# A seven-product unit in three accumulators, and a chunk's final products tied behind the accumulators' evictions

## The chip, the cores and the metric

The kernel runs on one core of one Trainium2 chip. The metric is the device time of one execution in microseconds (us), the median of several runs. Engines: PE is TensorE (matrix products into PSUM), DVE is VectorE, ACT is ScalarE, POOL is GpSimd, SP is SyncE, which here only issues DMAs. Each engine works through its own instructions in order.

## The reference

A trunk of two layers over x (1 x 2048 x 1024, float32), each `x <- x + mixer(RMSNorm(x))`, and a last RMSNorm. Layer A's mixer is a gated linear recurrence (RG-LRU) of width 1536. Layer B's is a short gated convolution:

```
u = einsum('bsd,dc->bsc', h, w_in)            # 1024 -> 4 x 1536
bg, cg, xv, gate = the four parts of u
y = bg * causal_depthwise_conv(cg * xv, conv_w)
out = einsum('bsc,cd->bsd', y * silu(gate), w_out)
```

Results must hold float32 accuracy; the kernel multiplies float32 as pairs of float16 (a high and a low part), three matmuls for one product.

## The kernel before, in words

All activations are held transposed, channels on the 128 partitions and 512 positions of the sequence along the row; such a 512-wide piece of the sequence is a chunk, two chunks a half. There are four chunks, 0 to 3.

Layer B's in-projection (`in_B`, `in_proj`, `unit`) makes 24 units of 256 output channels, each for both halves: 48 units. A unit is a 2 x 2 block product (output channels by chunks), done with seven block products instead of eight, after Strassen and Winograd: A11, S1, S2, A12, S4, S3 and A22 name the weight operand, and each meets one operand of the normalised x. A block product is four times three matmuls of 128x128 by 128x512, all into one PSUM accumulator (`product`, `mm3`). Accumulators come from a ring of six (`acc_tile`). The four results d[0,0], d[0,1], d[1,1], d[1,0] are sums of these products. Some sums are formed by letting further products grow in the same accumulator, others by adding an accumulator to a result in SBUF. Before, `unit` does it so:

- A11 grows in p; ACT copies p to d10 (L549). S1 is taken into r; DVE adds it to d10, giving d11 (`plus`, L539).
- The last product of the unit before is made here (`flush`): A22 grows in that unit's q, and DVE adds q to d10.
- S2 into a new q; DVE adds to d11, giving d01. A12 grows in p; ACT copies p to d00 (L565), which is finished.
- S4 into a new r; DVE adds it to d01, finished. S3 grows in q; DVE adds it to d11, finished. The final A22 in q waits for the next unit.

So a unit takes four accumulators, DVE evicts five times and ACT twice. A matmul that lets a product grow in an accumulator must wait until the eviction that reads the accumulator before it is over. Finished results go on to ACT (SiLU, L1020), POOL (products, L973 to L1049), and squares on ACT (L767, for the scale of the next operands).

Beside this, DVE and ACT split the next unit's weights into high and low halves (`split`, L420, L421), POOL forms the sums of weights (L484), and DVE does the convolution (L1005, L1009) and the evictions (L539).

Layer B's out-projection (`OutSums.run`) does the same seven products at a larger scale: for each half of the sequence, seven names, four row blocks q each, 28 products of 18 matmuls (6 operand blocks by 3). The first half's order is S1, S4, A12, A11, S2, S3, A22; the second's A11, S2, S3, A22, A12, S1, S4, the last two in half widths. A11, S2, S3 and A22 of one q grow in one accumulator. After each product DVE adds the accumulator to the residual x (`add_to_x`, L1428), one product late (`lag(1)`). Operands are loaded by SP (`fetch_to`) and split by ACT and DVE (L1117, L1118) some products ahead.

When all row blocks of a chunk are in, `endB` ends it: the sum of squares is turned into the factor `inv` of the last RMSNorm, and the chunk's eight blocks are multiplied with it (L1706), two of them on POOL and six on DVE, and stored. For chunks 0 and 1 `inv` is spread over the partitions by two DMAs issued from POOL's queue: `rd<-r` writes it to DRAM (L252), `inv<-rd` reads it back to all partitions (L253). In the first half chunk 1 is finished by S3's products and chunk 0 by A22's. The steps of an ending are put off by a count of products (`defer`, `tick`): for chunks 0 and 1 the sums at the fourth, the eight multiplications at the ninth (L1710).

What sets the order on an engine: the program is laid out when the kernel is built, by a simulation of time (`schedule_with_timeline_sim=True`) that takes instructions as they become ready in it, by priority. `after(a, b)` adds an order alone: a is laid out behind b, without any wait at run time. `evac_last` holds the last eviction of an accumulator; before, only the earlier out stage of layer A sets it.

Of the kernel before, what the change touches and what calls it, by code (L numbers as in the profile page):

```python
# [10 lines left out]
AF = mybir.ActivationFunctionType  # L11
ALU = mybir.AluOpType
# [34 lines left out]
def trunk(ctx, tc, xT, xn, prm, wa, ga, oa, wb, ob, out):  # L47
    nc = tc.nc
    v, s, g, sp = nc.vector, nc.scalar, nc.gpsimd, nc.sync
# [145 lines left out]
    def et(name, dt=F32):  # L195
        return buf(wk, "e", name, NE, dt)
# [95 lines left out]
    def inv_between(acc, inv, queue=None):  # L292

        ss = ps.tile([P, 4], F32, tag="g", name="ss", bufs=2)[:, 0 : acc.shape[1] // P]
        with tc.high_priority(PR):
            sums_of(acc, ss, pe_last[0])
        if not queue:
            yield
        with tc.high_priority(PR):
            inv_from(ss, inv, queue, s.copy, pe_last[0])  # L300
        yield
# [196 lines left out]
    def mm3(acc, wh, wl, xh, xl, start, stop, behind=None):  # L498
        kw = dict(skip_group_check=True)
        ins = nc.tensor.matmul(acc, wh, xh, start=start, stop=False, **kw)  # L500
        if behind is not None:
            after(ins, behind)
        nc.tensor.matmul(acc, wh, xl, start=False, stop=False, **kw)  # L503
        return nc.tensor.matmul(acc, wl, xh, start=False, stop=stop, **kw)  # L504

    throttle, pe_last, blocks_last, evac_last = [None, None], [None], [None], [None]
# [5 lines left out]
    def acc_tile(name):  # L512
        return ps.tile([P, CH], F32, tag="acc", name=name, bufs=6)
# [3 lines left out]
    def flush():  # L517

        while pending:
            pending.pop(0)()  # L520

    def unit(w, ops, dest, done, end):

        undo = w["undo"]

        def product(acc, wn, xn, start, stop):
            for k in range(4):
                kk = slice(k * P, (k + 1) * P)  # L530
                t, x = w[wn], ops[xn, k]
                pe_last[0] = mm3(
                    acc, t[:, 0, kk], t[:, 1, kk], x[:, 0, :], x[:, 1, :],
                    start and k == 0, stop and k == 3,
                )

        def plus(out, acc, t):
            with tc.high_priority(1000):
                ins = v.scalar_tensor_tensor(  # L539
                    out=out, in0=acc, scalar=undo, in1=t, op0=ALU.mult, op1=ALU.add  # L540
                )
            throttle[:] = ins, ins

        p = acc_tile("p")
        product(p, "A11", "B11", True, False)
        yield
        d10, d11 = dest(1, 0), dest(1, 1)
        with tc.high_priority(1000):
            s.activation(d10, p, AF.Copy, scale=undo)  # L549
        r = acc_tile("r")  # L550
        product(r, "S1", "T1", True, True)
        plus(d11, r, d10)
        yield
        if pending:
            flush()
            yield
        q = acc_tile("q")
        product(q, "S2", "T2", True, False)
        d01 = dest(0, 1)
        plus(d01, q, d11)  # L560
        yield
        product(p, "A12", "B21", False, True)
        d00 = dest(0, 0)
        with tc.high_priority(1000):
            s.activation(d00, p, AF.Copy, scale=undo)  # L565
        done(0, 0, d00)
        yield
        r = acc_tile("r")
        product(r, "S4", "B22", True, True)
        plus(d01, r, d01)  # L570
        done(0, 1, d01)
        yield
        product(q, "S3", "T3", False, False)
        plus(d11, q, d11)
        done(1, 1, d11)
        yield

        def last():
            product(q, "A22", "T4", False, True)
            plus(d10, q, d10)  # L580
            done(1, 0, d10)
            end()

        pending.append(last)
# [56 lines left out]
    def defer(fn, steps):  # L641
        deferred.append([steps, fn])

    def tick(n=1):

        for d in list(deferred):
            d[0] -= n
            if d[0] <= 0:
                deferred.remove(d)
                d[1]()  # L650
# [432 lines left out]
    def after(ins, first):  # L1083
        tc.add_manual_dep(
            ins.ins, first.ins.name,
            mybir.DependencyInfo(mybir.DependencyClass.NoSync, mybir.DependencyReason.SCHED_ONLY),
            reason="order",
        )
# [214 lines left out]
    class OutSums:  # L1303
# [98 lines left out]
        def run(self, emit, end_chunk, ending):  # L1402

            late = []

            def lag(n):
                while len(late) > n:
                    late.pop(0)()
                    next(ending, None)

            def product(acc, half, name, q, ts):
                start = SEVEN[name][2]
                for k in range(KH):
                    w, x = self.wops[name, k], self.zops[half, name, k]
                    kk = slice(q * P, (q + 1) * P)
                    behind = None if ts is CHUNK else last_of.get("PE")
                    mm = mm3(
                        acc[:, ts], w[:, 0, kk], w[:, 1, kk], x[:, 0, ts], x[:, 1, ts],
                        start and k == 0, k == KH - 1, behind,
                    )  # L1420
                    last_of["PE"] = mm
                throttle[:] = throttle[1:] + [mm]
                pe_last[0] = mm

            def add_to_x(acc, half, name, q, ts, final):
                m, c = SEVEN[name][1]
                x = self.x[half, m, c, q]
                ins = v.scalar_tensor_tensor(  # L1428
                    out=x[:, ts], in0=acc[:, ts], scalar=zsc[half][:, 2:3], in1=x[:, ts],
                    op0=ALU.mult, op1=ALU.add,  # L1430
                )
                if final:
                    cc, d = 2 * half + c, ND * m + q
                    if emit(cc, d, x, ts, ins):
                        end_chunk(cc, ts)

            n = 0
            for half, order in enumerate(self.ORDERS):
                accs = {}
                steps = [(name, CHUNK) for name in order]  # L1440
                if half:
                    steps[5:] = [(name, ts) for ts in (FIRST, SECOND) for name in order[5:]]
                for p, (name, ts) in enumerate(steps):
                    if (half, p) == (0, 3):
                        self.scales(1)
                    dest = SEVEN[name][1]
                    final = not [o for o, _ in steps[p + 1 :] if o != name and SEVEN[o][1] == dest
                                 and ts is CHUNK]
                    chain = ("S" if name in ("S1", "S4") else "Z" if name == "A12" else "X")
                    for q in range(ND):  # L1450
                        self.fetch_to(n)
                        while self.splits and self.splits[0][0] <= n:
                            self.split()
                        if SEVEN[name][2]:
                            accs[chain, q] = acc_tile("acc")
                        a = accs[chain, q]
                        product(a, half, name, q, ts)
                        late.append(
                            lambda a=(a, half, name, q, ts, final): add_to_x(*a)
                        )  # L1460
                        lag(1)
                        tick(1 if ts is CHUNK else 0.5)
                        n += 1 if ts is CHUNK else 0.5
                    if ts is not CHUNK:
                        lag(0)
                lag(0)
# [33 lines left out]
    acc = et("sa")  # L1500
# [11 lines left out]
    for c in range(2):  # L1512
        for i in range(4):
            t = wk.tile([P, D], F32, tag="xn", name="xn", bufs=4)
# [180 lines left out]
    def endB(c, ts):  # L1695
        if ts is not CHUNK:
            defer(lambda: endings.append(last_chunk(c, ts)), 1 if ts is FIRST else 0)
            return
        iv = et("inv")

        def ended():
            yield from inv_between(sums[c], iv, g if c < 2 else None)
            for d in range(KB):
                f = kept[c, d]
                eng = g if d % 3 == 2 else v
                eng.tensor_tensor(out=f, in0=f, in1=iv, op=ALU.mult)  # L1706
                sp.dma_start(out[d * P : (d + 1) * P, c * CH : (c + 1) * CH], f)

        steps = ended()
        for n in (4, 9) if c < 2 else (2, 3, 4):  # L1710
            defer(lambda: next(steps, None), n)


# [144 lines left out]
```

## Time and profile before

| | us |
|---|---|
| median of 3 runs | 1998.85 (1995.98 to 1999.11) |
| the profiled execution | 1997.66 |
| its span, first to last instruction | 1995.4 |
| PE busy | 1959.1 (98%) |
| DVE busy | 1257.5 (63%) |
| ACT busy | 1002.9 (50%) |
| POOL busy | 604.5 (30%) |
| mean granted TensorE clock | 0.994 |
| layer B's in-projection | about 868.8 to 1756.9 of the span |

Busy time is the time in which an engine's datapath works. Matmuls are pipelined and their ends are modelled, so single matmuls overlap in the records; the time from start to start is their pace. A wait is the idle time of an engine just before an instruction, with what ended it. In the rows below, times count from the span's start.

### The profile page before, as it was taken

To read this page: it belongs to the slowest core of one execution; us is meant where nothing else is said; L and a number is where in the kernel's file an instruction comes from. 1 tells how busy PE (TensorE), PEld (TensorE's weight loads), DVE (VectorE), ACT (ScalarE), POOL (GpSimd) and SP (SyncE) were. 2 spreads that over 40 slices of the span, in tenths; PEclk is the share of its full clock that TensorE was granted. 3 is DMA by queue.
4 is the path that set the end of the run, shared out by engine and by line. 5 is a ranking of instruction groups with operands and counts; after the bars stand their busy time and mean duration, and the time that the engine had idled before them with its cause. 6 is when DMAs were issued, how large, how long until landed. Compare 5 with 4: busy or idle time off the path is not lost.

```text
span 1995.4 us, 25154 instructions
## 1 busy us (share of the span) xinstructions
PE 1959.1 (98%) x9064; PEld 914.7 (46%) x9064; DVE 1257.5 (63%) x2137; ACT 1002.9 (50%) x1816; POOL 604.5 (30%) x486
## 2 busy tenths in 40 slices
PE   8999999999999999999999999999999999999988
PEld 3444444444444444444444444444444444444436
DVE  7977666667575745479647657658547438554455
ACT  7878786868584623155443343443432432435332
POOL 0001010101010311134553574664644544512221
PEclk9999999999999999999999999999999999999989
DMA  9111313052204824422141241232221120596442
GB/s 316 46 62 49 98 45 103 31 174 67 82 11 138 274 69 159 101 80 73 60 148 32 85 159 60 89 133 84 74 85 33 53 74 22 204 365 223 137 153 85
DMA packets 130957, 216.25 MB, mean 108 GB/s; under 512 B 13200, under 2 KB 41488, under 8 KB 130832
## 3 DMA queue, kind: packets, MB, share of 16 engines
q1 hardware_dynamic: 130384, 213.58, 32.4%
q8 instruction: 71, 1.16, 0.2%
q0 software_dynamic: 448, 1.06, 0.2%
q14 instruction: 54, 0.44, 0.1%
HBM read 152.19 MB, written 62.40 MB: 108 GB/s over the span
## 4 chain that ended last, share of the span: by engine, by line
PE 87%; DVE 6%; ACT 2%; DMA 2%; issue 2%; POOL 0%; SPq 0%; DVEq 0%; ACTq 0%; POOLq 0%
PE acc L500 14%; PE acc L503 14%; PE acc L504 14%; PE q L500 6%; PE q L504 6%; PE q L503 6%; PE p L504 4%; PE p L500 4%; PE p L503 4%; PE r L500 4%; PE r L504 4%; PE r L503 4%; PE pg L878 3%; DVE cg L1009 1%; DVE wc L421 1%
## 5 line engine op out<-in xcount | busy, mean ns | idle before, releaser
L503 PEld LDWEIGHTS <-wc 128*128 128x128 f16 x2096 | 205.1, 98 | 261.7 <-issue 27.5
L500 PEld LDWEIGHTS <-wc 128*128 128x128 f16 x2096 | 208.0, 99 | 253.3 <-issue 18.5
L504 PEld LDWEIGHTS <-wc 128*128 128x128 f16 x2096 | 205.2, 98 | 257.9 <-issue 14.5
L503 PE MATMUL acc<-op,wc 128*128 128x512 f16 x752 | 285.5, 380 | 2.8 <-DVE op L313 2.8
L504 PE MATMUL acc<-op,wc 128*128 128x512 f16 x752 | 285.7, 380 | 0.0
L500 PE MATMUL acc<-op,wc 128*128 128x512 f16 x752 | 283.3, 380 | 1.3 <-ACT op L311 1.3
L500 PE MATMUL q<-op,wc 128*128 128x512 f16 x576 | 216.5, 379 | 4.6 <-DVE ed L539 2.5
L903 POOL TENSOR_TENSOR u<-fixed,u 128x512 f32<-128x512 f32 x48 | 51.3, 1091 | 556.4 <-ACT fixed L900 556.4
L503 PE MATMUL q<-op,wc 128*128 128x512 f16 x576 | 218.3, 379 | 0.0
L504 PE MATMUL q<-op,wc 128*128 128x512 f16 x576 | 218.0, 379 | 0.0
L421 DVE SCALAR_TENSOR_TENSOR wc<-ws,fixed,wc 128x512 f16<-128x512 f32 x104 | 101.3, 979 | 87.6 <-ACT wc L420 79.5
L504 PE MATMUL p<-op,wc 128*128 128x512 f16 x384 | 145.5, 379 | 0.8 <-DVE wc L421 0.8
L503 PE MATMUL p<-op,wc 128*128 128x512 f16 x384 | 145.5, 379 | 0.0
L500 PE MATMUL p<-op,wc 128*128 128x512 f16 x384 | 145.5, 379 | 0.0
L500 PE MATMUL acc<-zs,wf 128*128 128x512 f16 x384 | 145.5, 379 | 0.0
L503 PE MATMUL acc<-zs,wf 128*128 128x512 f16 x384 | 145.5, 379 | 0.0
L504 PE MATMUL r<-op,wc 128*128 128x512 f16 x384 | 145.5, 379 | 0.0
L503 PE MATMUL r<-op,wc 128*128 128x512 f16 x384 | 145.5, 379 | 0.0
L500 PE MATMUL r<-op,wc 128*128 128x512 f16 x384 | 145.5, 379 | 0.0
L500 PE MATMUL acc<-op,wf 128*128 128x512 f16 (+1 forms) x384 | 136.2, 355 | 9.2 <-DVE xo L1428 9.2
L504 PE MATMUL acc<-zs,wf 128*128 128x512 f16 x384 | 145.2, 379 | 0.0
L503 PE MATMUL acc<-op,wf 128*128 128x512 f16 (+1 forms) x384 | 136.1, 354 | 0.0
(197 smaller groups left out, 3507.2 us busy)
## 6 DMA issues: line engine op xcount, KB each, us to landing
wr<-in_wb SPq DMA_DIRECT2D x104, 256.0 KB, 3.6
xs<-in_xT SPq DMA_DIRECT2D x48, 256.0 KB, 5.5
z<-sg SPq DMA_DIRECT2D x48, 256.0 KB, 2.0
zr<-z SPq DMA_DIRECT2D x48, 256.0 KB, 5.2
zr<-zT SPq DMA_DIRECT2D x48, 256.0 KB, 5.3
wr<-in_wa SPq DMA_DIRECT2D x44, 256.0 KB, 4.2
zB<-ed SPq DMA_DIRECT2D x36, 256.0 KB, 2.0
zT<-cg SPq DMA_DIRECT2D x36, 256.0 KB, 2.0
```

Source lines behind the costliest of these rows:

```text
L421: v.scalar_tensor_tensor(out=t[:, 1, :], in0=src, scalar=sw[:, 2:3], in1=t[:, 0, :], op0=ALU.mult, op1=ALU.subtract,)
L500: ins = nc.tensor.matmul(acc, wh, xh, start=start, stop=False, **kw)
L503: nc.tensor.matmul(acc, wh, xl, start=False, stop=False, **kw)
L504: return nc.tensor.matmul(acc, wl, xh, start=False, stop=stop, **kw)
L878: ins = nc.tensor.matmul(pg, gw[m][:, oo], u, start=True, stop=True)
L903: g.tensor_tensor(out=u, in0=w, in1=u, op=ALU.mult)
L1009: v.scalar_tensor_tensor(out=t, in0=tap(k), scalar=wc(k), in1=t, op0=ALU.mult, op1=ALU.add,)
```

## The change

Two parts. In `unit`, the seven products grow in three accumulators: A11, S2, S3 and A22 in p, S1 and S4 in r, A12 in q. `taken` lets ACT copy an accumulator to a result; `plus` lets DVE add an accumulator to a result that is there. ACT evicts four times a unit and DVE three times; results are allocated where they are first written.

In the last out stage, each eviction is noted in `evac_last`, the multiplications by `inv` are laid out behind the last one noted, and for chunks 0 and 1 they come at the tenth product instead of the ninth.

```
-        def plus(out, acc, t):
+        def taken(m, c, acc):
+            with tc.high_priority(1000):
+                s.activation(d[m, c], acc, AF.Copy, scale=undo)
+
+        def plus(m, c, acc):
             with tc.high_priority(1000):
                 ins = v.scalar_tensor_tensor(
-                    out=out, in0=acc, scalar=undo, in1=t, op0=ALU.mult, op1=ALU.add
+                    out=d[m, c], in0=acc, scalar=undo, in1=d[m, c], op0=ALU.mult, op1=ALU.add
                 )
             throttle[:] = ins, ins
-
+            done(m, c, d[m, c])
...
         product(p, "A11", "B11", True, False)
         yield
-        d10, d11 = dest(1, 0), dest(1, 1)
-        with tc.high_priority(1000):
-            s.activation(d10, p, AF.Copy, scale=undo)
+        d[0, 0] = dest(0, 0)
+        taken(0, 0, p)
         r = acc_tile("r")
-        product(r, "S1", "T1", True, True)
-        plus(d11, r, d10)
+        product(r, "S1", "T1", True, False)
+        d[1, 1] = dest(1, 1)
+        taken(1, 1, r)
         yield
         if pending:
             flush()
             yield
+        product(p, "S2", "T2", False, False)
+        d[0, 1] = dest(0, 1)
+        taken(0, 1, p)
+        yield
         q = acc_tile("q")
-        product(q, "S2", "T2", True, False)
-        d01 = dest(0, 1)
-        plus(d01, q, d11)
-        yield
-        product(p, "A12", "B21", False, True)
-        d00 = dest(0, 0)
-        with tc.high_priority(1000):
-            s.activation(d00, p, AF.Copy, scale=undo)
-        done(0, 0, d00)
-        yield
-        r = acc_tile("r")
-        product(r, "S4", "B22", True, True)
-        plus(d01, r, d01)
-        done(0, 1, d01)
-        yield
-        product(q, "S3", "T3", False, False)
-        plus(d11, q, d11)
-        done(1, 1, d11)
+        product(q, "A12", "B21", True, True)
+        plus(0, 0, q)
+        yield
+        product(r, "S4", "B22", False, True)
+        plus(0, 1, r)
+        yield
+        product(p, "S3", "T3", False, False)
+        plus(1, 1, p)
         yield
 
         def last():
-            product(q, "A22", "T4", False, True)
-            plus(d10, q, d10)
-            done(1, 0, d10)
+            product(p, "A22", "T4", False, True)
+            d[1, 0] = dest(1, 0)
+            taken(1, 0, p)
+            done(1, 0, d[1, 0])
             end()
...
+                evac_last[0] = ins
                 if final:
...
-                eng.tensor_tensor(out=f, in0=f, in1=iv, op=ALU.mult)
+                after(eng.tensor_tensor(out=f, in0=f, in1=iv, op=ALU.mult), evac_last[0])
...
-        for n in (4, 9) if c < 2 else (2, 3, 4):
+        for n in (4, 10) if c < 2 else (2, 3, 4):
```

## Rows read from the trace of the kernel before

**Rows 1.** The page's engine totals: busy us, share of the span, instructions.

```profile
PE 1959.1 (98%) x9064; PEld 914.7 (46%) x9064; DVE 1257.5 (63%) x2137; ACT 1002.9 (50%) x1816; POOL 604.5 (30%) x486
```

**Rows 2.** PE's waits, whole span: who waited for whom, total us, times, longest.

```profile
PE acc L500 <- DVE xo L1428: 9.2, 1, 9.2
...
PE q L500 <- DVE ed L539: 2.5, 2, 1.6
...
PE q L500 <- DVE fixed L107: 1.0, 1, 1.0
...
PE q L500 <- DVE pb L539: 0.9, 1, 0.9
PE p L504 <- DVE wc L421: 0.8, 1, 0.8
```

**Rows 3.** DVE's timeline: start, us, line, operation, out<-in, count, idle before and its end.

```profile
1887.99 0.73 DVE L1428 SCALAR_TENSOR_TENSOR xo<-acc,fixed,xo 128x512 f32<-128x512 f32 x1
1888.65 0.73 DVE L1118 SCALAR_TENSOR_TENSOR op<-zr,fixed,op 128x512 f16<-128x512 f32 x1
1902.27 5.84 DVE L1706 TENSOR_TENSOR xo<-xo,inv 128x512 f32<-128x512 f32 x6 [12.88 <-DMA inv<-rd]
...
1908.69 0.74 DVE L1428 SCALAR_TENSOR_TENSOR xo<-acc,fixed,xo 128x512 f32<-128x512 f32 x1
...
1913.32 0.74 DVE L1428 SCALAR_TENSOR_TENSOR xo<-acc,fixed,xo 128x512 f32<-128x512 f32 x1
```

**Rows 4.** PE's timeline around the long wait.

```profile
1899.87 0.38 PE L504 MATMUL acc<-op,wf 128*128 128x512 f16 x1
1909.48 0.58 PE L500 MATMUL acc<-op,wf 128*128 128x512 f16 x1 [9.23 <-DVE xo L1428]
...
1913.70 0.40 PE L503 MATMUL acc<-op,wf 128*128 128x512 f16 x1
...
1915.44 0.38 PE L500 MATMUL acc<-op,wf 128*128 128x512 f16 x1
```

**Rows 5.** Windows: stretch, busy PE, PEld, DVE, ACT, POOL, granted clock, DMA share, GB/s.

```profile
1910.00:1912.00 2.00, 2.00 (x7) 0.60 (x6) 2.00 (x5) 1.05 (x2) 0.00 (x0) 0.50 0.97 318
```

**Rows 6.** POOL's timeline in the last out stage.

```profile
1876.25 3.45 POOL L1706 TENSOR_TENSOR xo<-xo,inv 128x512 f32<-128x512 f32 x2 [2.75 <-DMA inv<-rd]
1887.07 0.80 POOL L252 DMA_DIRECT2D rd<-r  x1 [7.36 <-DVE r L249]
1898.01 0.55 POOL L253 DMA_DIRECT2D inv<-rd  x1 [10.15 <-DMA rd<-r]
```

**Rows 7.** DMA issues, 1850 to 1930: count, KB each, median us to landing.

```profile
rd<-r POOLq DMA_DIRECT2D x2, 2.0 KB, 9.9
```

**Rows 8.** Groups by line and form, whole span: count, busy us, mean ns, idle before.

```profile
L539 DVE SCALAR_TENSOR_TENSOR ed<-q,fixed,ed 128x512 f32<-128x512 f32 x72 | 53.7, 747 | 59.5 <-PE q L504 59.3
...
L549 ACT ACTIVATE ed<-p,fixed 128x512 f32<-128x512 f32 x24 | 16.3, 679 | 27.0 <-PE p L504 27.0
```

**Rows 9.** Windows in layer B's in-projection: all of it, and two crowded places.

```profile
868.80:1756.90 888.10, 882.74 (x4128) 404.69 (x4127) 560.18 (x817) 356.65 (x721) 451.52 (x359) 1.00 0.27 90
885.00:960.00 75.00, 72.29 (x338) 32.88 (x337) 73.47 (x112) 38.24 (x79) 29.66 (x25) 1.00 0.18 57
1090.00:1120.00 30.00, 27.51 (x129) 12.44 (x127) 27.02 (x34) 10.89 (x20) 19.32 (x14) 1.00 0.36 115
```

**Rows 10.** ACT's timeline in the second crowded place.

```profile
1112.92 0.63 ACT L1020 ACTIVATE th<-ed 128x512 f32<-128x512 f32 x1 [6.65 <-DVE ed L539]
...
1116.67 0.67 ACT L549 ACTIVATE ed<-p,fixed 128x512 f32<-128x512 f32 x1
```

**Rows 11.** PE's timeline there: the last matmul of that unit's S1.

```profile
1113.96 0.38 PE L504 MATMUL r<-op,wc 128*128 128x512 f16 x1
```

**Rows 12.** ACT's waits in layer B's in-projection: total us, times, longest.

```profile
ACT ed L565 <- PE p L504: 79.8, 20, 9.7
ACT fixed L767 <- POOL ed L1033: 64.6, 24, 5.6
```

More of the change, by code (lines that the diff above doesn't have):

```diff
@@ L535, in product @@
                 )
-        def plus(out, acc, t):
+        def taken(m, c, acc):
+            with tc.high_priority(1000):
+                s.activation(d[m, c], acc, AF.Copy, scale=undo)
+        def plus(m, c, acc):
             with tc.high_priority(1000):
                 ins = v.scalar_tensor_tensor(
-                    out=out, in0=acc, scalar=undo, in1=t, op0=ALU.mult, op1=ALU.add
+                    out=d[m, c], in0=acc, scalar=undo, in1=d[m, c], op0=ALU.mult, op1=ALU.add
                 )
             throttle[:] = ins, ins
+            done(m, c, d[m, c])
+        d = {}
         p = acc_tile("p")
```

## The prediction

> **What bounds the kernel now.** I read the page's line of engine totals first: TensorE (PE) is busy 1959.1 us of a span of 1995.4 [rows 1]. So at most 36.3 us can come off without fewer matmuls, and the change takes no matmul away. The question is only which idle time of PE it touches. The view of PE's waits gives the list [rows 2]: one wait of 9.2 us for DVE line 1428, an accumulator's addition to x in the last out stage; and in layer B's in-projection four rows, five waits, of 2.5 + 1.0 + 0.9 + 0.8 = 5.2 us, all for DVE. What is left lies at the kernel's start and end, which the change leaves alone.
>
> Then DVE's timeline around the long wait [rows 3]. At 1887.99 DVE evicts an accumulator, and with one split more it is through at 1889.4. The next it does is six multiplications of a finished chunk by `inv` (L1706), which wait 12.88 us for the DMA that brings `inv`; they run 1902.27 to 1908.11. Four accumulators stood ready meanwhile, evicted in a bunch from 1908.69 to 1913.32. PE's own timeline has the other side [rows 4]: the last matmul of S2 ends at 1900.25 (1899.87 + 0.38), the next starts at 1909.48, 9.23 us later. It is S3's first, which grows in the accumulator that S2's first row block has left, so it needs that eviction, the one at 1908.69. The idle time costs twice: the granted clock is 0.50 in 1910 to 1912 [rows 5], the lower of TensorE's two levels (1.2 of 2.4 GHz), after PE had stood for those 9 us, and the first ten matmuls take 4.22 us (1909.48 to 1913.70), where eight at the full clock take 1.74 (1913.70 to 1915.44), or 0.2175 each. Ten at that pace would be 2.18, so 2.04 us are lost to the lower clock. The stall's price is **9.23 + 2.04 = 11.3 us**.
>
> **Change 1, the tied products.** Chunk 0 is finished when half 1 begins. Its step of products is emitted at the tenth product now (ninth before). One product is 18 matmuls, 3.9 us by the 0.2175. Second half: A11 is products 1 to 4, S2 5 to 8, S3 9 to 12, A22 13 to 16. At the tenth the last eviction emitted is that of the ninth, S3's first, and the new tie puts DVE's six products behind it. Without the stall that product ends at 1900.25 + 3.9 = 1904.2 and is evicted by 1904.9. `inv` lands by 1902.27 [rows 3], so DVE need not wait; six products in 5.84 us end at 1910.8. Queued behind them: the eviction of product 10 (ready at 1908.1), needed by product 14, A22's second, which starts at 1900.25 + 5 x 3.9 = 1919.8. That leaves 8 us for it and for the splits of operands that stand in the same queue. Nothing on PE is late; the 11.3 us go. What is late next is only the output store, 3 us later than before and 85 us ahead of the end.
>
> Chunk 1, finished four products earlier, gets the same tie: its step comes at the second half's sixth product and stands behind the eviction of S2's first (ended 1900.25 - 3 x 3.9 = 1888.6). Its `inv` is there long before: POOL multiplied with it at 1876.25 [rows 6]. DVE is then busy with it until 1888.6 + 0.7 + 5.8 = 1895.1; the eviction behind it (ready 1892.4) is needed by product 10, at 1904.2. Nine us of cover.
>
> Two queues are passed on the way. POOL does two of the eight multiplications of a chunk, 3.45 us, and also issues both DMAs of the round trip, the second of which waits for the first: issued 1887.07, next step 1898.01 [rows 6]. Chunk 1's two products were ahead of both; tied behind 1888.6 they may come behind the second, near 1898.6, and end at 1902. SP issues the stores in order, so loads behind such a store could stand some 10 us. The x blocks and z blocks loaded there are asked for three products ahead or more, and an eviction that comes late has another three or four products of accumulator cover, 12 us or more. I take zero; the bounds are 0 and the price of the old wait, 9.2 us. No gain below zero: PE has no other wait here to lose.
>
> One rule bears on how safe this is. The row first: the 2 KB transfer `rd<-r` takes 9.9 us in the median [rows 7], and in this instance 10.9 from its issue to the next step of POOL's queue. The Trainium skill, "DMA: Bandwidth & Descriptors", section "Anatomy of one DMA — SWDGE (gpsimd) path", puts such a transfer at about 2.0 us fixed plus its bytes over 436 GB/s. By that, an estimate, `inv` (2 KB, then 256 KB) would have landed at 1887.07 + 2.0 + 2.6 = 1891.7, its products would have been over before 1900.25, and the kernel before could not have stalled; the tie would then have 12 us in hand. The trace contradicts the page. By the rows the margin is 1904.2 - 1902.3 = 1.9 us, and on that the second rival rests.
>
> The same tie touches chunk 2, near 1965, where six products stand before two half-width evictions. They now go a product of half width (2 us) later; nothing on PE waits there today. I take 0, with bounds -1 and +3 us, since the chain to the end passes through DVE soon after.
>
> **Change 2, the three accumulators.** A unit has seven products of 12 matmuls, 2.6 us each; there are 48 units. Before, DVE evicts five times a unit and ACT twice; after, DVE three times and ACT four. DVE loses 96 x 0.747 = 71.7 us, ACT gains 96 x 0.679 = 65.2 [rows 8]. In the stage, 888.1 us, DVE goes from 560.2 to 488.5 busy, ACT from 356.7 to 421.9 [rows 9]. On average neither bounds, but the average hides the places: DVE is busy 73.47 of 75 us in 885 to 960 and 27.02 of 30 in 1090 to 1120 [rows 9], and there the 5.2 us of PE waits lie. A unit lasts 18.2 us, so 1.49 us less a unit takes 6 us out of the first place and 2.5 out of the second, against single waits of at most 1.6 [rows 2]. One of them, 0.8, is for the weight split L421 that follows the same queue. I take 4 of the 5.2 as gone.
>
> What it adds is waits of PE for ACT. S2 is added to A11's accumulator once ACT has read it, with two products between (S1 and the last product of the unit before): 5.2 - 0.7 = 4.5 us of cover. S3 on S2's: A12 and S4 between, 4.5 again. S4 on S1's: three between. The final A22 stays behind DVE's eviction, two products as before. Is ACT ever 4.5 us late? The nearest row is its present eviction of A11. The worst I found is at 1116.67 [rows 10]. PE's S1 product ended at 1113.96 + 0.38 = 1114.3 [rows 11], A11's 2.6 earlier, at 1111.7; ACT came 4.9 late, 0.4 beyond the cover. Behind what? ACT had waited 6.65 us for a late DVE eviction [rows 10], and that lateness shrinks. Its other habit is the square in line 767, which waits for POOL 24 times, 64.6 us in all, 5.6 at most [rows 12]. With 96 new evictions, most behind 2.7 us on average, I take 1 us of new PE waits; bounds 0 (none beyond the cover) and 10 (ten waits, each half the length of the longest there is, 1 us past the cover, or fewer and longer). Destinations are taken later in their rings, which can only ease them. Net **-3 us**, between -5 and +5.
>
> **Sum.** The profiled execution took 1997.66 us, its span and 2.3 around it. 1997.66 - 11.3 - 3 = 1983.4. The median of the runs shown is 1998.85, 1.2 above the profiled one, so runs of the changed kernel may centre up to 1 us above the sum: I say **1984**.
>
> **Rivals.**
> First, ACT eats the gain of layer B and more: out stage as forecast, but the new readers cost what DVE gave back, up to +5: 1997.66 - 11.3 + 0 to 5 = 1986.4 to 1991.4. For it: in the crowded places ACT and DVE wait for one another [rows 10]. Against: the 4.5 us of cover and an ACT below half busy. 0.22.
> Second, the tie doesn't remove the stall, it moves it: `inv` of chunk 0 lands later, because the stores of chunk 1 now fall into its round trip (1889 to 1897), and DVE stands before product 10's eviction. It needs `inv` some 10 us later than 1902. At its old size the wait would return: 1997.66 - 3 = 1994.7. For it: the margin of 1.9 us and DMAs of 10 us. Against: the cover of 8 us behind it. 0.08.
> Third, slower: ACT's line 767 stands in front of an eviction. If all 24 of its waits came at the longest, 5.6 us, before an eviction with 4.5 of cover, each would cost PE 1.1: 26 us, or 1997.66 - 11.3 + 26 = 2012. It decides from 11 such waits on. For it: ACT's queue is in order and POOL is late every b unit. Against: the mean is 2.7 us, and at 20 of the 24 present evictions of A12's sum into `ed` ACT is there first and waits for PE [rows 12]. 0.06.
> The forecast keeps 0.64.
>
> **Range and chances.** The low end is everything: 16.5 off, and a run 1.5 below the profiled one: 1979.5. The high end takes the first rival whole: 1991.5. Outside lie the second and third and some scatter, under 0.2. About 0.2%, 4 us, is what a measurement can tell from no change. Faster: forecast and first rival, 0.86; within: the second, 0.08; slower: the third, 0.06.
>
> **What would show it.** PE's waits have no row for L1428 over 1 us; granted clock 1.00 from 1900 to 1950 (shifted by the gain); DVE's products of chunk 0 follow S3's first eviction with no wait for `inv`. In layer B: DVE near 490 us busy, ACT near 420, PE's waits for DVE under 2 us and for ACT about 1. I am wrong if PE waits several us for an ACT eviction of p, if L1706 again waits for `inv` ahead of accumulators that PE needs, or if a new wait for an operand split appears in the out stage.

## The result, and the profile after

The changed kernel takes 1982.0 us (1980.3 to 1984.6, 4 runs) beside 1998.0 us for the kernel before: ratio 0.9922, 95% interval 0.9905 to 0.9939, so 12 to 19 us faster. Timed again beside the experiments below: 0.9924, 0.9912 to 0.9937. The forecast was 1984, range 1979.5 to 1991.5.

The profiled execution took 1984.61 us, 13.05 less than the profiled one of before. In us, from the two traces and from that of the second timing (`changed again`):

| stretch | before | changed | changed again |
|---|---|---|---|
| start to layer B's first product | 868.8 | 870.6 | 868.1 |
| from there to PE's last matmul | 1119.7 | 1105.2 | 1106.1 |
| behind it | 6.9 | 6.9 | 6.9 |

The first stretch holds nothing of the change; over the thirteen profiles of this study it lies between 866.0 and 871.9, and with 1.7 us it is what the profiled pair hides of the gain. The second lost 14.5 and 13.6 us.

The waits of PE that answer to [rows 2], lines shifted by the diff (`taken` is L539 on ACT, `plus` L543 on DVE, the last out stage's eviction L1430, its products L1709): who waited for whom, us, times, longest.

```profile
PE p L500 <- ACT wc L420: 1.2, 1, 1.2
...
PE p L500 <- DVE pb L543: 0.8, 1, 0.8
...
PE p L504 <- DVE wc L421: 0.4, 1, 0.4
...
PE p L500 <- DVE ed L543: 0.3, 1, 0.3
```

No row for L1430 is there. Layer B's 5.2 us became 2.7, and the one row that names ACT is for a split of weights, not for a copy out of an accumulator. With the 9.2 us wait and the 2.0 us at the lower clock this makes 11.3 + 2.5 = 13.8 us, which agrees with the stretch's 13.6 and 14.5. Windows of layer B's in-projection and of the place where the wait was (stretch, then PE, PEld, DVE, ACT, POOL busy, granted clock, DMA share, GB/s) answer to [rows 9] and [rows 5]:

```profile
868.00:1757.00 889.00, 886.27 (x4146) 406.31 (x4145) 500.71 (x723) 420.62 (x823) 450.26 (x362) 1.00 0.27 91
...
1886.00:1950.00 64.00, 64.00 (x354) 34.51 (x353) 35.79 (x56) 27.69 (x46) 13.67 (x10) 1.00 0.48 155
```

DVE went from 560 to 501, ACT from 357 to 421, and PE is busy all through the second window, at the full clock.

Now DVE's timeline in the last out stage of the changed kernel, beside [rows 3]. Before that, rows of the kernel before that I should have read and did not, from the same view of its DVE:

```profile
1859.83 0.75 DVE L1428 SCALAR_TENSOR_TENSOR xo<-acc,fixed,xo 128x512 f32<-128x512 f32 x1 [2.48 <-PE acc L504]
...
1864.52 0.75 DVE L1428 SCALAR_TENSOR_TENSOR xo<-acc,fixed,xo 128x512 f32<-128x512 f32 x1 [2.53 <-PE acc L504]
...
1868.40 0.75 DVE L1428 SCALAR_TENSOR_TENSOR xo<-acc,fixed,xo 128x512 f32<-128x512 f32 x1 [2.48 <-PE acc L504]
1876.20 4.04 DVE L1706 TENSOR_TENSOR xo<-xo,inv 128x512 f32<-128x512 f32 x3 [7.05 <-DMA inv<-rd]
...
1883.30 0.73 DVE L1428 SCALAR_TENSOR_TENSOR xo<-acc,fixed,xo 128x512 f32<-128x512 f32 x1
...
1884.62 0.73 DVE L1428 SCALAR_TENSOR_TENSOR xo<-acc,fixed,xo 128x512 f32<-128x512 f32 x1
...
1886.61 0.16 DVE L249 RECIPROCAL r<-r 128x4 f32<-128x4 f32 x1
1886.70 0.71 DVE L1428 SCALAR_TENSOR_TENSOR xo<-acc,fixed,xo 128x512 f32<-128x512 f32 x1
```

The last eviction of the first half is the one at 1859.83: it is the last with a square of its result behind it on ACT. So 1864.52 and 1868.40 are the second half's products 1 and 2, 1883.30 to 1887.99 its products 3 to 6, and 1908.69, behind the long wait, is product 7. Behind product 2 DVE turns to chunk 1's products and waits 7.05 us for their `inv`, with product 3 ready. Only at 1886.61 does it come to the reciprocal from which chunk 0's `inv` is made. The changed kernel:

```profile
1877.06 0.17 DVE L249 RECIPROCAL r<-r 128x4 f32<-128x4 f32 x1
1879.66 0.75 DVE L1430 SCALAR_TENSOR_TENSOR xo<-acc,fixed,xo 128x512 f32<-128x512 f32 x1 [2.43 <-PE acc L504]
1880.33 4.06 DVE L1709 TENSOR_TENSOR xo<-xo,inv 128x512 f32<-128x512 f32 x6
...
1890.97 1.41 DVE L1120 SCALAR_TENSOR_TENSOR op<-zr,fixed,op 128x512 f16<-128x512 f32 x2 [5.25 <-ACT op L1119]
1892.30 0.74 DVE L1430 SCALAR_TENSOR_TENSOR xo<-acc,fixed,xo 128x512 f32<-128x512 f32 x1
...
1895.60 0.74 DVE L1430 SCALAR_TENSOR_TENSOR xo<-acc,fixed,xo 128x512 f32<-128x512 f32 x1
1896.27 5.18 DVE L1709 TENSOR_TENSOR xo<-xo,inv 128x512 f32<-128x512 f32 x6
```

Chunk 1's six products stand behind product 5 (S2's first, 1879.66), chunk 0's behind product 9 (S3's first, 1895.60), neither waits for `inv`, and the reciprocal comes at 1877.06. POOL's timeline, beside [rows 6], shows `inv` of chunk 0 landing 7 us sooner, at 1895.31 instead of 1902.27 (1.2 us of it because this trace reaches the out stage's sums of squares sooner, at 1874.77 instead of 1875.97):

```profile
1877.52 0.77 POOL L252 DMA_DIRECT2D rd<-r  x1 [4.05 <-DVE r L249]
1878.32 2.50 POOL L1709 TENSOR_TENSOR xo<-xo,inv 128x512 f32<-128x512 f32 x2
1888.47 0.59 POOL L253 DMA_DIRECT2D inv<-rd  x1 [7.65 <-DMA rd<-r]
1895.31 3.18 POOL L1709 TENSOR_TENSOR xo<-xo,inv 128x512 f32<-128x512 f32 x2 [6.25 <-DMA inv<-rd]
```

### The profile page after: what moved, and what is told of

Read it like the earlier page. It is cut to its first block, busy times and chain, and to the rows that moved or that the text cites. A ratio compares the mean times of both kernels' runs of the same rounds, so it can differ in the third digit from the quotient of the medians.

```text
span 1982.7 us, 25189 instructions
## 1 busy us (share of the span) xinstructions
PE 1959.7 (99%) x9064; PEld 915.8 (46%) x9064; DVE 1194.6 (60%) x2041; ACT 1063.5 (54%) x1912; POOL 597.6 (30%) x486
## 4 chain that ended last, share of the span: by engine, by line
PE 90%; DVE 6%; ACT 2%; DMA 1%; issue 1%; POOL 0%; SPq 0%; DVEq 0%; ACTq 0%
PE acc L504 15%; PE acc L503 15%; PE acc L500 15%; PE p L504 8%; PE p L500 8%; PE p L503 8%; PE r L500 4%; PE r L504 4%; PE r L503 4%; PE pg L880 3%; PE q L504 2%; PE q L500 2%; PE q L503 2%; DVE op L313 1%; DVE u L843 1%
## 5 line engine op out<-in xcount | busy, mean ns | idle before, releaser
L504 PEld LDWEIGHTS <-wc 128*128 128x128 f16 x2096 | 205.2, 98 | 257.4 <-issue 14.2
L500 PE MATMUL p<-op,wc 128*128 128x512 f16 x768 | 290.7, 379 | 2.3 <-ACT wc L420 1.2
L503 PE MATMUL p<-op,wc 128*128 128x512 f16 x768 | 291.1, 379 | 0.0
L504 PE MATMUL p<-op,wc 128*128 128x512 f16 x768 | 290.6, 379 | 0.4 <-DVE wc L421 0.4
L421 DVE SCALAR_TENSOR_TENSOR wc<-wr,fixed,wc 128x512 f16<-128x512 f32 x122 | 106.9, 894 | 78.0 <-ACT wc L420 66.1
L504 PE MATMUL acc<-op,wf 128*128 128x512 f16 (+1 forms) x384 | 135.3, 352 | 0.0
L503 PE MATMUL acc<-op,wf 128*128 128x512 f16 (+1 forms) x384 | 135.3, 352 | 0.0
L500 PE MATMUL acc<-op,wf 128*128 128x512 f16 (+1 forms) x384 | 135.3, 352 | 0.0
L230 POOL TENSOR_TENSOR sa<-sa,sq 128x512 f32<-128x512 f32 x48 | 67.1, 1398 | 224.9 <-ACT sq L229 177.7
```

What stands on the lines that cost most here:

```text
L230: squared[0] = eng.tensor_tensor(out=acc, in0=acc, in1=sq, op=ALU.add)
L421: v.scalar_tensor_tensor(out=t[:, 1, :], in0=src, scalar=sw[:, 2:3], in1=t[:, 0, :], op0=ALU.mult, op1=ALU.subtract,)
```

## The experiments

All are edits of the kernel before or of the changed one; ratios are to the kernel before, timed beside them, medians in us.

| run | median | ratio (95%) | PE's wait for the eviction |
|---|---|---|---|
| tie and tenth product only | 1988.3 | 0.9943 (0.9929 to 0.9957) | none |
| three accumulators only | 1995.6 | 0.9987 (0.9978 to 0.9995) | 9.4 |
| tie, ninth product | 1983.3 | 0.9926 (0.9914 to 0.9938) | 0.7 |
| tenth product, no tie | 1996.4 | 0.9986 (0.9977 to 0.9995) | 10.2 |
| chunk 1 untied | 1981.8 | 0.9923 (0.9910 to 0.9937) | none |
| chunk 0 untied | 1986.5 | 0.9945 (0.9931 to 0.9958) | 3.0 |
| `inv` by PE, untied | 1987.2 | 0.9949 (0.9934 to 0.9965) | none |
| copies by DVE | 1991.8 | 0.9970 (0.9960 to 0.9981) | none |
| copies made twice | 1989.7 | 0.9959 (0.9945 to 0.9972) | none |
| first tap on ACT | 1980.5 | 0.9914 (0.9900 to 0.9927) | none |
| changed again | 1983.0 | 0.9924 (0.9912 to 0.9937) | none |

**The two parts apart.** To the kernel before:

```
+                evac_last[0] = ins
-                eng.tensor_tensor(out=f, in0=f, in1=iv, op=ALU.mult)
+                after(eng.tensor_tensor(out=f, in0=f, in1=iv, op=ALU.mult), evac_last[0])
-        for n in (4, 9) if c < 2 else (2, 3, 4):
+        for n in (4, 10) if c < 2 else (2, 3, 4):
```

> Only change 1 (the tie and the tenth product); layer B's units are those of before. Theory: the two parts add. The out stage loses its long wait and the time at the lower clock (11.3 us by the trace of before; 10.9 us is what the stage lost in the changed kernel's trace), layer B keeps its 5.2 us of waits. Time: about 11 us under before, 1987, ratio 0.9945. PE's waits: no row for the eviction L1428 over 1 us, the five waits of layer B unchanged. Rival: what removed the stall is the new layout of everything behind layer B's units, not the tie; then a wait for L1428 of several us is still here and the time is 1990 or more.

And the changed kernel with these lines taken back, `unit` left as changed:

> Only change 2 (three accumulators, four evictions a unit on ACT); the last out stage is that of before. Theory: layer B's in-projection takes 3.6 us less, as it does in the changed kernel's trace (884.5 for 888.1), and the out stage keeps a wait for L1428 of 9 us and a granted clock of 0.50 behind it. Time: about 3.5 us under before, 1994.5, ratio 0.998. Rival: the units alone already take the stall away or halve it; then the time is 1990 or less.

Measured: -11.4 us (8.6 to 14.2) and -2.6 us (1.0 to 4.4). Together 14.0, inside the interval of both at once. With the tie alone layer B keeps its five waits; with the accumulators alone the long wait stays, 9.4 us. Both theories hold and the parts add.

**What of change 1 does it.** In the changed kernel, first the ninth product with the tie, then the tenth without:

```
-        for n in (4, 10) if c < 2 else (2, 3, 4):
+        for n in (4, 9) if c < 2 else (2, 3, 4):
```

> The changed kernel with the multiplications emitted at the ninth product instead of the tenth, tie kept. Theory: the tie does it; chunk 1's products then stand behind A11's fourth eviction and chunk 0's behind S2's fourth, one product earlier each, and DVE waits up to 4 us for chunk 0's inv with S3's first still to be evicted, which PE does not need for another four products. Time as the changed kernel, 1982, within 1 us. Rival: the margin is as thin as inv's landing in the changed trace (0.4 us before the products start) makes it look, and one product earlier brings back a wait of several us: 1985 to 1990.

```
-                after(eng.tensor_tensor(out=f, in0=f, in1=iv, op=ALU.mult), evac_last[0])
+                eng.tensor_tensor(out=f, in0=f, in1=iv, op=ALU.mult)
```

> The changed kernel without the tie, multiplications still emitted at the tenth product. Theory: a later step alone does not hold them; chunk 1's products go ahead of A11's third eviction again and DVE waits there for their inv (7 us in the kernel before), which delays the reciprocal of chunk 0 and its round trip; chunk 0's products end up ahead of accumulators that PE needs. PE waits for L1428 by 5 to 9 us, time 1988 to 1993. Rival: one product later is enough, the tie is idle: no wait, time 1982.

The tie does it. At the ninth product DVE waits 7.58 us for chunk 0's `inv`, where up to 4 were expected, its evictions come up to 11.6 us late, and PE waits 0.7: the time is the changed kernel's, but the cover is used up. That is what the tenth product buys.

```profile
1895.70 5.84 DVE L1709 TENSOR_TENSOR xo<-xo,inv 128x512 f32<-128x512 f32 x6 [7.58 <-DMA inv<-rd]
...
1902.79 0.74 DVE L1430 SCALAR_TENSOR_TENSOR xo<-acc,fixed,xo 128x512 f32<-128x512 f32 x1
```

Without the tie DVE's timeline is that of before, and so is the time but for layer B's gain. The theory had the direction and not the size: PE waits 10.2 us and not 5 to 9, and 1996.4 lies above its 1988 to 1993.

```profile
1875.29 4.05 DVE L1709 TENSOR_TENSOR xo<-xo,inv 128x512 f32<-128x512 f32 x3 [7.34 <-DMA inv<-rd]
...
1885.70 0.16 DVE L249 RECIPROCAL r<-r 128x4 f32<-128x4 f32 x1
...
1902.04 5.83 DVE L1709 TENSOR_TENSOR xo<-xo,inv 128x512 f32<-128x512 f32 x6 [13.56 <-DMA inv<-rd]
...
1908.46 0.74 DVE L1430 SCALAR_TENSOR_TENSOR xo<-acc,fixed,xo 128x512 f32<-128x512 f32 x1
```

**The two links.** In the changed kernel the tie is left out for chunk 1 (below), then for chunk 0:

```
-                after(eng.tensor_tensor(out=f, in0=f, in1=iv, op=ALU.mult), evac_last[0])
+                ins = eng.tensor_tensor(out=f, in0=f, in1=iv, op=ALU.mult)
+                if c != 1:
+                    after(ins, evac_last[0])
```

> The changed kernel with the tie on chunk 0's products alone; chunk 1's are free again. Theory: two links make the long wait. Chunk 1's products, placed too early, hold DVE until their inv lands; with that they delay the reciprocal of chunk 0 by some 9 us and so its round trip (reciprocal at 1886 instead of 1877). Then chunk 0's products, placed ahead of S2's third eviction, wait for the late inv. Cutting the second link alone must do: DVE waits 7 us for chunk 1's inv and again for chunk 0's, but behind S3's first eviction, which leaves PE 2 to 3 us or none to wait. Time 1982 to 1985. Rival: the first link alone costs PE its time; wait for L1428's place of 5 us or more, 1988 and up.

> The changed kernel with the tie on chunk 1's products alone; chunk 0's are free again and go ahead of S2's third eviction. Theory: chunk 0's reciprocal stays early (1877), its inv lands near 1895, DVE stands from about 1886 to 1895 and multiplies until 1900; S2's third eviction ends near 1901.5, where PE needs it at 1899: a wait of 2 to 3 us at the full clock. Time 1984 to 1986. Rival: chunk 1's tie alone is enough (no wait, 1982), or it does nothing (9 us and the lower clock, 1993).

With chunk 1 untied the reciprocal of chunk 0 is late and DVE waits for both factors, 7.72 and 6.68 us, and PE for neither, for chunk 0's products stand behind product 9. It was near: product 10's eviction, the next behind them, ended at 1905.55 (1904.81 + 0.74), and product 14, which needs it, started at 1906.28.

```profile
1871.19 4.05 DVE L1709 TENSOR_TENSOR xo<-xo,inv 128x512 f32<-128x512 f32 x3 [7.72 <-DMA inv<-rd]
...
1881.60 0.16 DVE L249 RECIPROCAL r<-r 128x4 f32<-128x4 f32 x1
...
1898.38 5.85 DVE L1709 TENSOR_TENSOR xo<-xo,inv 128x512 f32<-128x512 f32 x6 [6.68 <-DMA inv<-rd]
...
1904.81 0.74 DVE L1430 SCALAR_TENSOR_TENSOR xo<-acc,fixed,xo 128x512 f32<-128x512 f32 x1
```

With chunk 0 untied its products go ahead of product 7's eviction (S2's third), the reciprocal is early (1875.04), and PE waits 3.0 us, as expected; the time, 1986.5, is 0.5 us above what was expected:

```profile
1875.04 0.17 DVE L249 RECIPROCAL r<-r 128x4 f32<-128x4 f32 x1
...
1893.50 5.85 DVE L1709 TENSOR_TENSOR xo<-xo,inv 128x512 f32<-128x512 f32 x6 [3.07 <-DMA inv<-rd]
...
1899.28 0.74 DVE L1430 SCALAR_TENSOR_TENSOR xo<-acc,fixed,xo 128x512 f32<-128x512 f32 x1
```

So the wait of before is made by two links: chunk 1's products, placed too early, delay the reciprocal for chunk 0's factor (10.6 us behind the start of chunk 0's sums on PE in the kernel before, 2.3 in the changed one), and chunk 0's products hold DVE until the factor comes. Cutting the second is enough; cutting the first alone leaves 3 us.

**Is it the round trip?** The kernel before, untied:

```
-            yield from inv_between(sums[c], iv, g if c < 2 else None)
+            yield from inv_between(sums[c], iv, None)
-        for n in (4, 9) if c < 2 else (2, 3, 4):
+        for n in (4, 5, 9) if c < 2 else (2, 3, 4):
```

> The kernel before, untied and at the ninth product, but inv of chunks 0 and 1 spread over the partitions by matmuls with ones on PE (as chunk 2's already is) instead of the two DMAs. Theory: what DVE stood for is the round trip; without it the products are ready where they are laid out and the six of them hold DVE for 4 to 6 us only. No wait for L1428 over 1 us; PE gets two times 0.9 us of small matmuls more. Time: 1998.2 - 11.3 + 1.8 = 1988.7. Rival: the six products themselves are the trouble, wherever inv comes from; then a wait of 4 us or more stays, 1993 and up.

1987.2: no wait of PE for the eviction, though the six products still go ahead of evictions, which come up to 5.4 us late. They stand one product earlier than before, behind products 1 and 5. DVE waits 2.90 us for `inv`, twice, instead of 7.05 and 12.88. What PE stood for was the DMAs, not the products.

```profile
1867.79 5.85 DVE L1706 TENSOR_TENSOR xo<-xo,inv 128x512 f32<-128x512 f32 x6 [2.90 <-ACT inv L265]
1873.56 0.74 DVE L1428 SCALAR_TENSOR_TENSOR xo<-acc,fixed,xo 128x512 f32<-128x512 f32 x1
...
1885.02 5.86 DVE L1706 TENSOR_TENSOR xo<-xo,inv 128x512 f32<-128x512 f32 x6 [2.90 <-ACT inv L265]
```

**What of change 2 does it.** In the changed kernel the copies go to DVE:

```
-                s.activation(d[m, c], acc, AF.Copy, scale=undo)
+                v.tensor_scalar(out=d[m, c], in0=acc, scalar1=undo, scalar2=None, op0=ALU.mult)
```

> The changed kernel with the four copies of a unit made by DVE instead of ACT: three accumulators, seven evictions a unit on DVE (five in the kernel before, three in the changed one). Theory: layer B's gain comes from the engine that evicts, not from the number of accumulators. DVE gets 192 x 0.75 = 144 us more, 500 to 644 us of the 888 in layer B's in-projection, and its queue, full already in the crowded places (885 to 960, 1090 to 1120, 1240 to 1260), runs late there: PE waits 10 to 25 us for DVE. Time 1990 to 2005. Rival: the accumulators or the later places in the rings give the gain; then time within 3 us of the changed kernel's 1982.

1991.8, about 9 us above the changed kernel (ratio 0.9970 beside 0.9922 and 0.9924): with three accumulators but DVE evicting seven times a unit PE's waits for DVE evictions in layer B come to 8.0 us in six waits, 2.5 the longest (10 to 25 were expected), and 2.0 more for weights; the mean granted clock is 0.84 from 920 to 930.

```profile
PE p L500 <- DVE ed L539: 3.8, 3, 2.3
PE r L500 <- DVE pb L539: 2.5, 1, 2.5
PE p L500 <- ACT wc L420: 2.0, 1, 2.0
PE p L500 <- DVE ed L543: 1.1, 1, 1.1
...
PE p L500 <- DVE pb L543: 0.6, 1, 0.6
```

So three accumulators alone don't give the gain when DVE makes all the evictions: this run is slower than the tie with the old units (ratio 0.9970 beside 0.9943). But DVE evicts more here than in the kernel before, and whether three accumulators with the old split of evictions would gain anything wasn't run. That the gain is the engine's alone is likely and not shown.

**How near is ACT?** Every copy is made twice:

```
                 s.activation(d[m, c], acc, AF.Copy, scale=undo)
+                s.activation(d[m, c], acc, AF.Copy, scale=undo)
```

> The changed kernel with each of the four copies of a unit made twice by ACT, the second over the first: 192 x 0.68 = 131 us more on ACT, 420 to 551 us of the 888 in layer B's in-projection, and every eviction done 0.7 us later. It asks how near ACT is to being late. Theory: of the 4.5 us between an eviction's start and the product that needs its accumulator nearly all is spare; PE waits 1 to 4 us more than in the changed kernel. Time 1983 to 1986. Rival (the slower case of the forecast): ACT's queue runs late as a whole, behind its waits for POOL and DVE, and PE pays in many units: 10 us or more, 1992 and up.

1989.7, 6.7 us above the changed kernel beside it: more than the theory's 1 to 4 us, less than the rival's 10. PE's waits in layer B are 8.6 us instead of 3.1 there, and none is for a copy; they are for the weights' split on ACT and for DVE evictions:

```profile
PE p L500 <- ACT wc L420: 4.1, 2, 3.8
PE p L500 <- DVE pb L544: 3.7, 2, 1.9
...
PE p L500 <- DVE ed L544: 0.8, 1, 0.8
```

The name of ACT misleads in the longest of them, 3.8 us: ACT itself had stood idle for 6.92 us before that split, for the small DVE instruction that makes the weights' scale (L397). It was DVE's queue that was late there. By which path the doubled copies delay DVE wasn't followed.

```profile
922.37 0.72 ACT L420 ACTIVATE wc<-wr,fixed 128x512 f16<-128x512 f32 x1 [6.92 <-DVE fixed L397]
```

The other part is the clock. The 3.8 us wait ends at 923.1, and the mean granted clock is 0.66 in the windows 920 to 930, a mixture of the two levels, 1.2 and 2.4 GHz:

```profile
915.00:920.00 5.00, 4.33 (x21) 1.76 (x18) 5.00 (x7) 0.45 (x1) 3.29 (x3) 1.00 0.14 50
920.00:925.00 5.00, 1.86 (x5) 0.69 (x6) 4.87 (x11) 2.63 (x5) 0.00 (x0) 0.66 0.02 4
925.00:930.00 5.00, 5.00 (x17) 1.89 (x15) 3.06 (x5) 3.91 (x8) 2.60 (x3) 0.66 0.61 209
930.00:935.00 5.00, 5.00 (x25) 2.25 (x23) 5.00 (x9) 5.00 (x14) 0.09 (x1) 1.00 0.17 53
```

From 925 to 930 PE is busy throughout and makes 17 matmuls, where it makes 25 in the next 5 us at the full clock.

**One step on.** The first tap of the convolution moves to ACT:

```
-                        v.tensor_scalar(
-                            out=t, in0=tap(0), scalar1=wc(0), scalar2=None, op0=ALU.mult
-                        )
+                        s.activation(t, tap(0), AF.Copy, scale=wc(0))
```

> The changed kernel with the convolution's first tap (L1005 of the kernel before, 48 times 0.67 us on DVE) made by ACT. An attempt to go on: the 2.7 us of waits that layer B has left lie where DVE is still full (70 of 75 us in 885 to 960). Theory: the waits for DVE evictions (0.8 and 0.3 us) go, those for the weights' splits (1.2 and 0.4) go in part. Time 1 to 2 us under the changed kernel. Rival: ACT then stands in its queue for POOL's product before the tap (DVE does so 13 times, 17.8 us) and evicts late: 0 to 5 us over.

1980.5 beside 1983.0 for the changed kernel on the same chip. Layer B's waits are 2.2 us (1.3 and 0.9) for 3.1 there. It is faster than the kernel before beyond doubt; the intervals of the two ratios overlap, so that it beats the changed kernel is likely and not shown.

> The changed kernel once more, beside the others, for a closer interval and to see which part of the profiled difference was the start of that one execution. Theory: median 1982 within 1 us, ratio 0.992; layer B's in-projection 884.5 us and the part from its end to PE's end 220.7 us as in the profile before, while the first 870 us differ by a few us from run to run with the granted clock of the first 60 us. Rival: the 2 to 3 us by which the timed gain exceeds the profiled one lie in layer B or the out stage; then these two stages are shorter here.

1983.0 and 0.9924. Layer B and the out stage repeat within 1 us; the start differs from execution to execution, and with it the mean granted clock of the first 70 us (0.93 where it ends at 870.6 and 871.9, 1.00 where it ends at 866.0). The timed gain, 15 to 16 us, has 13.6 to 14.5 inside its interval; nothing more has to be explained.

## Why the prediction was right, and where not

**The price of the long wait** was right: 11.3 us in the forecast, 11.4 with the tie alone.

**Which product it was** was wrong. I put PE's wait on S3's first product and the ready accumulator on S2's first; counting evictions from 1859.83 it is S3's third (product 11) that waited for S2's third (product 7), and S3's first had ended by 1896.4, not 1904.2. With the late `inv` (1902.27) the margin I gave as 1.9 us was therefore -5.9 us, and DVE would have waited. The cover behind it was as wrong: A22's second (product 14) was due three products after 1900.25, at 1912 and not 1919.8, so that of the 8 us some 2.5 were there. It did no harm for two reasons: the next eviction behind the products is needed only by A22's second, as the forecast said (chunk 1 untied shows it, 6.68 us of DVE waiting and none of PE), and the tie on chunk 1 brought `inv` forward. The first had 0.7 us in hand and the second I had not seen: that the long wait went whole was in part luck.

**The tie on chunk 1** I took for a move without worth, with 9 us of cover. It is the first link: its 7.05 us of waiting stood ahead of chunk 0's reciprocal. On this the second rival was built (`inv` later, because chunk 1's stores fall into its round trip); it came 7 us earlier instead. Of the round trip, the first DMA took what the row said: 10.95 us from `rd<-r` to the next DMA, 10.94 before. The second took longer: from its issue to the products 6.8 us (1888.47 to 1895.31), 4.3 before (1898.01 to 1902.27). The same holds in every run with the two DMAs: 5.9 to 7.5 us where chunk 1's stores go out during chunk 0's round trip, 3.7 to 4.3 where they were issued before it. So the rival named a real cost, some 2.5 us, and missed that the round trip would start 9.5 us earlier (reciprocal at 1877.06 instead of 1886.61). The Trainium skill, "DMA: Bandwidth & Descriptors", section "Anatomy of one DMA — SWDGE (gpsimd) path", fits a DMA of this queue as 2.0 us fixed plus its bytes over 436 GB/s, by estimate 2.0 us for these 2 KB. Both traces contradict that: `rd<-r` took 9.9 us in the median to land before and 10.0 in the changed kernel.

**POOL and SP.** POOL's two products of chunk 1 slipped between the two DMAs, not behind them. SP's stores did hold back loads, as feared: eight stores over 10.86 us, and the next loads of operands only at 1890.58. But the wait of 13.14 us that ACT had there was not for those loads, since its splits began at 1890.21; the row names the landing of a store as what ended it. The kernel before has the like behind chunk 0's stores (17.71 us, to 1910.95). Why a split should wait for a store isn't shown.

```profile
1879.63 10.86 SPq L1710 DMA_DIRECT2D out_xT<-xo  x8
1890.58 1.71 SPq L1362 DMA_DIRECT2D zr<-zT  x2
...
1890.21 5.63 ACT L1119 ACTIVATE op<-zr,fixed 128x512 f16<-128x512 f32 x9 [13.14 <-DMA out_xT<-xo]
```

Through DVE's split (5.25 us, above) S2's third eviction came 4.9 us late, at 1892.30; PE needed it at 1898.89. The forecast's zero held with 5.9 us left.

**Change 2**, -3 us forecast: -2.6 timed alone; in that run's trace the waits are 2.2 us shorter and the stage 3.3. DVE 490 and ACT 420 forecast, 501 and 421 measured. In the changed kernel PE's waits that name DVE fell from 5.2 to 1.5 us, and one of 1.2 us names ACT, for a split of weights. It comes from DVE too: ACT had stood idle 7.82 us before that split, for the weights' scale (L397) in DVE's full queue:

```profile
923.16 0.72 ACT L420 ACTIVATE wc<-wr,fixed 128x512 f16<-128x512 f32 x1 [7.82 <-DVE fixed L397]
```

So of the waits that DVE makes 2.5 us went, not 4, and the new waits for ACT copies that I priced at 1 us are none. The two errors nearly cancel. That the weights' split would remain was named; it is now the largest of layer B's waits.

**The rivals.** The first (ACT takes the gain back) didn't come; at double the copies it would have: 131 us more of ACT cost 6.7 us, though through waits that end on DVE for the most part. The third put the price in line 767's wait; no wait of PE in the runs names a copy that stood behind it. The chance of "faster" was right; the median came 2 us under the forecast, within its range.

## What to carry to other kernels

An engine that works in order and is given, too early, an instruction whose input comes over a DMA loses not that wait but everything laid behind it; look for what else stands in that queue, above all the start of the next such round trip. Lay such consumers behind the work that the bottleneck engine needs next, and leave one product of cover beyond the round trip that the trace shows. An eviction can go to whichever engine has room at the crowded place; mean busy shares don't tell which. And follow a wait one step further back: the engine that it names may itself have stood for another.

## What was not expected of the hardware

Six multiplications on DVE took 4.06 us when POOL's two ran mostly before them (the changed kernel, at 1880.33) and 5.84 us when both engines started together (the kernel before, at 1902.27): 0.68 and 0.97 us each. The 2 KB transfer `rd<-r` kept POOL's next DMA waiting 9.4 to 10.9 us from its issue, all four times in the two traces, where 256 KB loads land in 3.6 to 5.5 us by the medians of the rows on the profile's page of the kernel before. Why it takes so long isn't shown.
